# Sliding-window attention by whole chunks in single PSUM banks, in a one-layer encoder step on one core

## The chip, the cores and the metric

The kernel runs on one core of one Trainium2 chip. A core has TensorE (PE in the profile, with its weight loads as PEld), VectorE (DVE), ScalarE (ACT), GpSimd (POOL) and SyncE (SP), on-chip memory for operands, and PSUM, the memory that TensorE writes, which this kernel divides into eight banks of 512 float32 values for each of 128 partitions. Each engine works through its own queue in order; DMA transfers are issued from such queues and run beside them. The metric is the device time of one execution, in microseconds (us).

## The reference

One layer of a hybrid encoder, in float32, over 1088 tokens: 1024 of a prompt and 64 new ones (the "sample"), width 1024. Two branches read one projection: retention (4 heads of 256) and sliding-window attention (SWA). Their gated sum is projected and added; then come cross-attention to 256 memory tokens and a SwiGLU network of width 2816. The part that matters here is the SWA of the mixer:

```python
def swa_attend(q, k, v, bias, sinks, valid):   # chunks of 64 queries; 16 heads in 2 groups; head width 64
    s = einsum('bnqhgd,bnkhd->bnhgqk', q, k) * (SWA_HD ** -0.5)
    s = s + bias                                # own chunk and the two before it: 192 keys
    if valid is not None:
        s = where(valid, s, NEG_INF)
    sink = sinks[:, :, None, None]
    m = maximum(max(s, axis=-1, keepdims=True), sink)
    e = exp(s - m)
    p = e / (sum(e, axis=-1, keepdims=True) + exp(sink - m))
    return einsum('bnhgqk,bnkhd->bnqhgd', p, v)

def merge_branches(ret_o, ret_g, swa_o, gate_a, gate_b, w_ret_out, w_swa_out, w_mix_out):
    a = (rms_norm(ret_o).reshape(B, S, -1) * silu(ret_g)) @ w_ret_out
    b = swa_o.reshape(B, S, -1) @ w_swa_out
    return (sigmoid(gate_a) * a + sigmoid(gate_b) * b) @ w_mix_out
```

There are 17 chunks of 64 queries, 16 of the prompt and one of the sample, whose keys come from a cache. The first two chunks have 64 and 128 keys, all others 192. `mem_kv` also makes the memory's values (`mv`), which are an output.

## The kernel before

`Kernel.run` goes through phases: the projection (with retention and the memory's keys and values beside it), `swa_phase`, `merge_swa`, cross-attention and the SwiGLU network. Large products are made in three fp32r matmuls: an operand is cut by `split` (L122) into a high part, cast by ScalarE (L123), and a low part, subtracted by VectorE (L124), and `mm3` (L153) multiplies high by high, high by low and low by high. In the profile these are the lines L156, L157 and L158. Matmuls of the attention are plain fp32 ones.

**The SWA stage**, `swa` (L927), runs from about 808 to 1000 us. A chunk's 16 heads go in two halves `hf`; in each half there are four tiles, `units`, `(v, i)`: v is the group of keys (two sets of 64 partitions), i the pair of heads. The stage has three steps:

- `scores(c, hf)` (L964): four fp32 products (L972; eight records, since the profile counts two for an fp32 matmul) into `pss`, a tile of two banks with one bank for each v; four VectorE reductions (L982) that add bias and find the row's extreme (`nm`); the sink's term `es` (L986); four ScalarE exponentials with row sums (L988) and one of the sink (L990); then VectorE adds (L991) and inverts (L992) the sums `den`, and GpSimd multiplies the probabilities by them: `t` (L994) for the first 128 keys, `e` (L999, two instructions) for the last 64.
- `turn(c, hf)` (L1003): values are transposed (L949, once per block of keys) into a `pd` bank and copied by ScalarE (L951); four transposes of `t` (L1011) into a bank `pt0`, copied out by ScalarE (L1015, `pT`); two transposes of `e` (L1022) into a bank `pt1`, copied out by VectorE (L1024).
- `weigh(c)` (L1028): eight fp32 products (L1035) of probabilities and values into `pout`, which VectorE copies to `osb` (L1039). Every second chunk is stored to `d_swa`.

PSUM's eight banks are used so: two for `pd` (one-bank tiles of the filler and the value transposes), two for `pss`, one `pt0`, one `pt1`, two `pout`.

**The filler.** Softmax work of VectorE, ScalarE and GpSimd takes longer than the products of a half, so TensorE is given other work between the steps: `filler` (L1151) makes pieces of 12 fp32r matmuls. The first four pieces finish the last head of the memory's values (`wq` by `ms`, 256 columns, scaled by ScalarE at L1167 and stored from GpSimd's queue at L1168 and L1169). All others are halves of a product of retention's output with `w_ret_out` (`ret` by `wq`; 384 columns for the first two blocks of tokens, 320 for the last), multiplied by a gate on VectorE (L1196). The `ret` operands come in three blocks of columns: block 0 was loaded and cast ahead, with its low parts made by `first_low` (L1116, L1120); blocks 1 and 2 are loaded, cast and subtracted by `later_operands` (L1122) in halves of four, when the filler reaches the steps in `extra`.

**What sets the order.** `in_order` (L911) fixes TensorE's order to that of the calls. The loop over half chunks i calls `weigh` of the chunk that ended with half i−1, `scores` of half i+2, `turn` of half i, and then one filler piece (at a few steps two). The other engines' queues are filled by a scheduler that simulates the program's times; `issue_after` and `high_priority` push single instructions. `marks` keeps, for each half, the instructions behind which `first_low` and `later_operands` are to stand.

Of the kernel before, what the change touches and what calls it, by code (L numbers as in the profile page):

```python
# [11 lines left out]
F32 = mybir.dt.float32  # L12
# [97 lines left out]
class Kernel:  # L110
# [781 lines left out]
    def swa_phase(self):  # L892
        with ExitStack() as ctx:
            filler = []

            def fill():


                pieces = self.filler()
                yield []  # L900
# [26 lines left out]
    def swa(self, ctx, fill):  # L927
        nc, tc, io = self.nc, self.tc, self.io
        if True:
# [15 lines left out]
            def values(lo):  # L945
                if lo not in vtok:
                    n = min(P, KC - lo)
                    pt = self.dense_psum()
                    self.last_mm = nc.tensor.transpose(pt[:n, :P], vT[:, lo:lo + n], self.ident).ins  # L949
# [6 lines left out]
            halves = [(c, hf) for c in range(17) for hf in range(2)]  # L956
# [7 lines left out]
            def scores(c, hf):  # L964
                ks, j0, nk = keys(c)
                if hf == 0 and c % 4 == 0 and 0 < c < 13:
                    self.load_queries(qTs, c + 4)
                qT = qTs[c // 4 % 2]
                pss = pw.tile([P, 2, 512], F32, tag="s", name="pss")
                for i in range(2):  # L970
                    for v in range(2):
                        self.last_mm = mm(pss[:, v, i * NKEY:i * NKEY + nk], qT[rows[v], 2 * hf + i, c % 4, :],  # L972
# [4 lines left out]
                ps = pss[:, :, :2 * NKEY].rearrange("p v (i n) -> p v i n", n=NKEY)  # L977
                bs = bias.rearrange("p (v h i) n -> p v h i n", v=2, h=2)
                nm = sw.tile([P, 2, 2], F32, tag="nm", name="nm")
                for v, i in units:  # L980
                    u = quad(self.minus)[:, v, i:i + 1]
                    nc.vector.tensor_tensor_reduce(t[:, v, i, :nk], ps[:, v, i, :nk], bs[:, v, hf, i, j0:], -0.125, u,  # L982
# [20 lines left out]
            def turn(c, hf):  # L1003
                ks, j0, nk = keys(c)
                if hf == 0:
                    live[c] = [values(ks + k0) for k0 in ((0, 64, P) if nk == NKEY else (0,))]
                (t, e), vt = live.pop((c, hf)), live[c]
                n = min(P, nk)
                pp = pw.tile([P, 512], F32, tag="pt0", name="pp")
                for j, (v, i) in enumerate(units):  # L1010
                    self.last_mm = nc.tensor.transpose(pp[:n, j * P:(j + 1) * P], t[:, v, i, :n], self.ident).ins  # L1011
                if hf == 0:
                    live[c, "T"] = [self.pw2.tile([P, 2, 512], F32, tag="pT0", name="pT"), self.pw2.tile([P, 512], F32, tag="pT1", name="pT")]
                pT = live[c, "T"][0][:n]
                nc.scalar.copy(pT[:, :, hf * 256:(hf + 1) * 256], pp[:n, :].rearrange("p (v i) -> p v i", v=2))  # L1015
                cs = [slice(h * 256, (h + 1) * 256) for h in range(2)]
                parts = [[(h, v, vt[0][:n], pT[:, v, cs[h]]) for h in range(2) for v in range(2)]]
                if nk == NKEY:
                    pp = pw.tile([P, 512], F32, tag="pt1", name="pp")
                    for i in range(2):  # L1020
                        x = e[:, i].rearrange("p r k -> p (r k)")
                        self.last_mm = nc.tensor.transpose(pp[:, i * P:(i + 1) * P], x, self.ident).ins  # L1022
                    pT = live[c, "T"][1]
                    nc.vector.tensor_copy(pT[:, hf * 256:(hf + 1) * 256], pp[:, :256])  # L1024
                    parts.append([(h, r ^ h, vt[2 - r][rows[r]], pT[rows[r], cs[h]]) for h in range(2) for r in (h, 1 - h)])
                live[c, "parts"] = parts

            def weigh(c, hf):  # L1028
                if hf == 0:
                    return  # L1030
                parts = live.pop((c, "parts"))
                po = pw.tile([P, 2, 512], F32, tag="out", name="pout")
# [14 lines left out]
            n = len(halves)  # L1047
            for i in range(-2, n):
                if i > 0:
                    self.in_order(lambda: weigh(*halves[i - 1]))  # L1050
                if i + 2 < n:
                    self.in_order(lambda: scores(*halves[i + 2]))
                if i >= 0:
                    self.in_order(lambda: turn(*halves[i]))
                for pieces in next(fill):
                    self.in_order(lambda: next(pieces, None))
                if i == -2:
                    with tc.high_priority(), tc.issue_after(self.last_operand):
                        self.tokens(vT, 1, "cvT")
                if i == 2:  # L1060
                    with tc.issue_after(self.last_operand):
                        self.load_queries(qTs, 4)
                if i == 8:
                    with tc.issue_after(self.last_operand):
                        keep()
            self.in_order(lambda: weigh(*halves[n - 1]))
            for pieces in next(fill):
                self.in_order(lambda: next(pieces, None))
# [82 lines left out]
    def filler(self):  # L1151

        nc, tc, io = self.nc, self.tc, self.io
        if True:
# [3 lines left out]
            for t in range(2):  # L1158
# [7 lines left out]
                with tc.high_priority():  # L1166
                    self.values_out = nc.scalar.mul(o, ps[:, :256], self.mtok[:, t:t + 1]).ins  # L1167
# [9 lines left out]
            extra = {2: (1, 0), 3: (1, 1), 5: (2, 0), 7: (2, 1)}  # L1177
            step = 0
            for m, c in order:
# [9 lines left out]
                for ps in self.pieces(u, rets, c0, n):  # L1189
                    if step in extra:  # L1190
                        i, j = extra.pop(step)
                        self.later_operands(*CH[i], halves[j])
# [641 lines left out]
```

## Time and profile before

| what | value |
|---|---|
| median of 3 runs | 2181.84 us (2179.26 to 2182.01) |
| profiled execution | 2183.19 us |
| its span in the trace | 2181.1 us |
| granted TensorE clock, mean | 0.995 |
| TensorE busy | 2142.3 us, 98% |
| VectorE, ScalarE, GpSimd busy | 1553.4, 876.4, 651.7 us |

A row of the timeline has the start, the duration as recorded, the engine, the line, the operation with its result and operands, the size, how many equal instructions in a row it stands for (x8), and in square brackets the idle time before it and what ended that. Records of one engine overlap a little, since an instruction starts before the one ahead of it has quite ended; the cost of one in a row of many is the distance between starts.

### The profile page before, as it was taken

To read this page: it belongs to the slowest core of one execution; us is meant where nothing else is said; L and a number is where in the kernel's file an instruction comes from. 1 tells how busy PE (TensorE), PEld (TensorE's weight loads), DVE (VectorE), ACT (ScalarE), POOL (GpSimd) and SP (SyncE) were. 2 spreads that over 40 slices of the span, in tenths; PEclk is the share of its full clock that TensorE was granted. 3 is DMA by queue.
4 is the path that set the end of the run, shared out by engine and by line. 5 is a ranking of instruction groups with operands and counts; after the bars stand their busy time and mean duration, and the time that the engine had idled before them with its cause. 6 is when DMAs were issued, how large, how long until landed. Compare 5 with 4: busy or idle time off the path is not lost. (4 is left out here: it accounts for less than half of the span.)

```text
span 2181.1 us, 41848 instructions
## 1 busy us (share of the span) xinstructions
PE 2142.3 (98%) x16389; PEld 2089.0 (96%) x16389; DVE 1553.4 (71%) x2824; ACT 876.4 (40%) x1898; POOL 651.7 (30%) x498
## 2 busy tenths in 40 slices
PE   8999999999999999999999999999999999999997
PEld 8999999999999997889999999999999999999997
DVE  8996868776687658665455555768777777787688
ACT  7344424344344447553233333333322322344343
POOL 1223233342344214430000000014565555514531
PEclk9999999999999999999999999999999999999999
DMA  6434354435344467326443111422333323294433
GB/s 208 154 131 114 114 152 125 137 111 159 103 160 164 166 206 246 118 80 219 124 155 120 40 49 59 146 87 91 121 124 116 105 96 120 94 331 128 135 107 119
DMA packets 181446, 290.84 MB, mean 133 GB/s; under 512 B 40290, under 2 KB 109314, under 8 KB 181250
## 3 DMA queue, kind: packets, MB, share of 16 engines
q1 hardware_dynamic: 176130, 278.18, 40.1%
q10 hardware_dynamic: 4608, 8.36, 1.0%
q8 instruction: 129, 2.11, 0.4%
q0 software_dynamic: 512, 1.64, 0.2%
q14 instruction: 67, 0.55, 0.1%
HBM read 196.95 MB, written 91.16 MB: 132 GB/s over the span
## 5 line engine op out<-in xcount | busy, mean ns | idle before, releaser
L124 DVE TENSOR_TENSOR wq<-raw,wq 128x512 fp32r<-128x512 f32 (+1 forms) x499 | 443.9, 893 | 134.8 <-ACT wq L123 131.4
L123 ACT CAST wq<-raw 128x512 fp32r<-128x512 f32 (+1 forms) x499 | 303.1, 614 | 567.1 <-PE pq L215 223.3
L212 PE MATMUL pq<-T,wq 128*128 128x272 f32 x1832 | 492.0, 288 | 4.9 <-ACT wq L123 3.3
L213 PE MATMUL pq<-T,wq 128*128 128x272 f32 x1832 | 492.9, 289 | 0.0
L213 PE MATMUL pq<-B,wq 128*128 128x272 f32 x1592 | 428.2, 289 | 2.9 <-DVE B L124 2.6
L212 PE MATMUL pq<-B,wq 128*128 128x272 f32 x1592 | 426.6, 288 | 0.5 <-ACT B L123 0.5
L190 POOL TENSOR_TENSOR raw<-raw 128x512 f32<-128x512 f32 (+1 forms) x59 | 86.0, 1458 | 1036.5 <-DVE rs_r L301 483.0
L215 PE MATMUL pq<-T,wq 128*128 128x272 f32 x1832 | 382.8, 289 | 1.5 <-DVE wq L124 1.5
L212 PEld LDWEIGHTS pq<-T,wq 128*128 128x128 f32 x1832 | 345.0, 188 | 6.7 <-ACT wq L123 3.1
L213 PEld LDWEIGHTS pq<-T,wq 128*128 128x128 f32 x1832 | 344.9, 188 | 1.2 <-issue 1.1
L215 PE MATMUL pq<-B,wq 128*128 128x272 f32 x1592 | 332.2, 289 | 0.0
L213 PEld LDWEIGHTS pq<-B,wq 128*128 128x128 f32 x1592 | 299.5, 188 | 4.3 <-DVE B L124 4.2
L212 PEld LDWEIGHTS pq<-B,wq 128*128 128x128 f32 x1592 | 299.4, 188 | 1.4 <-ACT B L123 0.9
L215 PEld LDWEIGHTS pq<-T,wq 128*128 128x128 f32 x1832 | 290.2, 190 | 2.6 <-DVE wq L124 1.8
L215 PEld LDWEIGHTS pq<-B,wq 128*128 128x128 f32 x1592 | 252.2, 190 | 0.5 <-issue 0.4
L259 DVE TENSOR_TENSOR u<-pq,u 128x544 f32<-128x544 f32 x177 | 127.2, 719 | 95.5 <-PE pq L215 95.4
L193 POOL TENSOR_TENSOR raw<-raw 128x512 f32<-128x512 f32 (+1 forms) x59 | 80.8, 1370 | 91.4 <-DVE wq L124 81.5
L598 DVE TENSOR_TENSOR stage<-pq,u 128x544 f32<-128x544 f32 x112 | 80.3, 717 | 36.9 <-PE pq L215 32.4
L191 POOL TENSOR_TENSOR raw<-raw 128x512 f32<-128x512 f32 (+1 forms) x59 | 88.8, 1505 | 3.6
L196 POOL TENSOR_TENSOR raw<-raw 128x512 f32<-128x512 f32 (+1 forms) x59 | 84.0, 1423 | 4.4
L1483 POOL TENSOR_TENSOR stage<-stage,rstd_f 128x544 f32<-128x544 f32 x40 | 63.9, 1607 | 39.1 <-ACT stage L1482 39.1
L156 PE MATMUL pd<-xc,wq 128*128 128x256 f32 (+1 forms) x256 | 74.5, 291 | 0.0
(383 smaller groups left out, 4548.4 us busy)
## 6 DMA issues: line engine op xcount, KB each, us to landing
hl<-d_op SPq DMA_DIRECT2D x85, 272.0 KB, 5.3
d_qkv<-stage SPq DMA_DIRECT2D x44, 272.0 KB, 2.7
d_op<-stage SPq DMA_DIRECT2D x44, 272.0 KB, 2.1
d_op<-ht SPq DMA_DIRECT2D x44, 272.0 KB, 3.3
raw<-w_gate SPq DMA_DIRECT2D x22, 512.0 KB, 3.6
raw<-w_up SPq DMA_DIRECT2D x22, 512.0 KB, 4.0
raw<-w_down SPq DMA_DIRECT2D x16, 512.0 KB, 4.8
d_gate<-stage ACTq DMA_DIRECT2D x28, 272.0 KB, 3.0
```

The costliest lines, as they stand in the source:

```text
L123: self.last_cast = self.nc.scalar.copy(hi, src).ins
L124: return self.nc.vector.tensor_tensor(out=lo, in0=src, in1=hi.bitcast(F32), op=ALU.subtract).ins
L156: mm(ps, wh, xh, start=start, stop=False)
L190: tt(out=a11, in0=a11, in1=a21, op=sub)
L191: tt(out=a21, in0=a21, in1=a22, op=add)
L193: tt(out=a11, in0=a22, in1=a11, op=sub)
L196: tt(out=a12, in0=a12, in1=a11, op=sub)
L212: mm(ps[:, c, :HC], w[:, 0, ks], x[:, 0, cs], start=start, stop=False)
L213: mm(ps[:, c, :HC], w[:, 0, ks], x[:, 1, cs], start=False, stop=False)
L215: self.last_mm = mm(ps[:, c, :HC], w[:, 1, ks], x[:, 0, c * HC:(c + 1) * HC], start=False, stop=stop).ins
L259: add = lambda out, a, b: nc.vector.tensor_tensor(out=out, in0=a, in1=b, op=ALU.add)
L598: nc.vector.tensor_tensor(out=o, in0=ps, in1=sb, op=ALU.add)
```

## The change

The stage goes by whole chunks instead of half chunks.

- *Scores in single banks.* `pss` becomes one tile of one bank for each v, from a ring of four "s" banks. A chunk's two halves take four tiles.
- *Turning.* The transposes of `t` take two more tiles of the same ring, one for each half; those of `e` go into the upper halves of the two banks of the chunk's `pout` tile, whose lower halves `weigh` writes. So `pt0` and `pt1` are gone, and `pout` is taken by `turn`. `e` is copied out once for a chunk instead of once for each half.
- *Values.* All new blocks of a chunk are transposed into one `pd` bank and then copied.
- *Order.* Scores(0), six pieces; then for each chunk c weigh(c−1), scores(c+1), the filler's pieces, turn(c), the filler's pieces. Before, a piece followed each half.
- *Copies first.* The copies by ScalarE out of the banks get high priority, and `marks` takes turn's copies, so that casts for the next columns stand behind them.
- *Filler.* The scaling of the memory's values goes from ScalarE to VectorE. Both halves of column block 1 are requested at step 3 instead of one each at steps 2 and 3.
- The loads of queries for chunks 4 to 7 and the storing of keys and values (`keep`) are called behind chunks 1 and 4.

In the changed program's queues, as built, TensorE has the same instructions. Four gate loads stand ahead of a query load on SyncE's queue. On GpSimd's the issues of the memory values' four stores stand ahead of the first chunk's normalising. On VectorE's the two scalings stand ahead of chunk 0's reciprocals, and the reciprocals of chunk 2 stand behind the reductions of chunk 3.

```diff
-            def values(lo):
-                if lo not in vtok:
-                    n = min(P, KC - lo)
+            def values(los):
+                new = [lo for lo in los if lo not in vtok]
+                if new:
                     pt = self.dense_psum()
-                    self.last_mm = nc.tensor.transpose(pt[:n, :P], vT[:, lo:lo + n], self.ident).ins
-                    vt = vtok[lo] = vts.pop(0)
-                    nc.scalar.copy(vt[:n, :], pt[:n, :P])
-                return vtok[lo]
+                    for j, lo in enumerate(new):
+                        n = min(P, KC - lo)
+                        self.last_mm = nc.tensor.transpose(pt[:n, j * P:(j + 1) * P], vT[:, lo:lo + n], self.ident).ins
+                    for j, lo in enumerate(new):
+                        n = min(P, KC - lo)
+                        vt = vtok[lo] = vts.pop(0)
+                        with tc.high_priority():
+                            nc.scalar.copy(vt[:n, :], pt[:n, j * P:(j + 1) * P])
+                return [vtok[lo] for lo in los]
...
-                pss = pw.tile([P, 2, 512], F32, tag="s", name="pss")
+                pss = [pw.tile([P, 512], F32, tag="s", bufs=4, name="pss") for v in range(2)]
...
+            def turn(c):
...
+                def most(hf):
+                    pp = pw.tile([P, 512], F32, tag="s", bufs=4, name="pp")
+                    t = live[c, hf][0]
+                    for j, (v, i) in enumerate(units):
+                        self.last_mm = nc.tensor.transpose(pp[:n, j * P:(j + 1) * P], t[:, v, i, :n], self.ident).ins
+                    with tc.high_priority():
+                        copied = nc.scalar.copy(first[:, :, cs[hf]], pp[:n, :].rearrange("p (v i) -> p v i", v=2)).ins
+                    self.marks.append((self.marks[-1][0], copied))
+                for hf in range(2):
+                    self.in_order(lambda: most(hf))
+                po = pw.tile([P, 2, 512], F32, tag="out", name="pout")
+                for hf, i in units if nk == NKEY else ():
+                    x = live[c, hf][1][:, i].rearrange("p r k -> p (r k)")
+                    self.last_mm = self.in_order(lambda: nc.tensor.transpose(po[:, hf, (2 + i) * P:(3 + i) * P], x, self.ident)).ins
...
+                    nc.vector.tensor_copy(rest.rearrange("p (h i) -> p h i", h=2), po[:, :, 256:])
...
-            n = len(halves)
-            for i in range(-2, n):
-                if i > 0:
-                    self.in_order(lambda: weigh(*halves[i - 1]))
-                if i + 2 < n:
-                    self.in_order(lambda: scores(*halves[i + 2]))
-                if i >= 0:
-                    self.in_order(lambda: turn(*halves[i]))
-                for pieces in next(fill):
-                    self.in_order(lambda: next(pieces, None))
...
+            self.in_order(lambda: scores(0))
...
+            filled()
+            for c in range(17):
+                if c:
+                    self.in_order(lambda: weigh(c - 1))
+                if c < 16:
+                    self.in_order(lambda: scores(c + 1))
+                filled()
+                self.in_order(lambda: turn(c))
+                filled()
...
-                    self.values_out = nc.scalar.mul(o, ps[:, :256], self.mtok[:, t:t + 1]).ins
+                    self.values_out = nc.vector.tensor_scalar(o, ps[:, :256], self.mtok[:, t:t + 1], None, ALU.mult).ins
...
-            extra = {2: (1, 0), 3: (1, 1), 5: (2, 0), 7: (2, 1)}
+            extra = {3: ((1, 0), (1, 1)), 5: ((2, 0),), 7: ((2, 1),)}
```

More of the change, by code (lines that the diff above doesn't have):

```diff
@@ new lines, in turn, with weigh @@
+                parts = [[(h, v, vt[0][:n], first[:, v, cs[h]]) for h in range(2) for v in range(2)]]
+                if nk == NKEY:
+                    rest = self.pw2.tile([P, 512], F32, tag="pT1", name="pT")
+                    nc.vector.tensor_copy(rest.rearrange("p (h i) -> p h i", h=2), po[:, :, 256:])
+                    parts.append([(h, r ^ h, vt[2 - r][rows[r]], rest[rows[r], cs[h]]) for h in range(2) for r in (h, 1 - h)])
+                live[c] = parts, po
+            def weigh(c):
+                parts, po = live.pop(c)
@@ L1190, in filler @@
                     if step in extra:
[L1191 to L1192 removed]
+                        for i, j in extra.pop(step):
+                            self.later_operands(*CH[i], halves[j])
                     step += 1
```

58 lines of the change are left out of this document (19 added, 39 removed).

## The prediction

> **What bounds the kernel now.** I read the page's busy times first, then the two windows tables over the stage that the change touches, then the timelines of TensorE and of the engines that feed it.
>
> ```profile
> PE 2142.3 (98%) x16389; PEld 2089.0 (96%) x16389; DVE 1553.4 (71%) x2824; ACT 876.4 (40%) x1898; POOL 651.7 (30%) x498
> 800.00:820.00 20.00, 18.17 (x131) 17.70 (x130) 9.57 (x31) 11.83 (x35) 2.23 (x4) 0.83 0.77 199
> 820.00:840.00 20.00, 18.13 (x122) 14.97 (x121) 17.75 (x59) 12.35 (x43) 5.78 (x8) 1.00 0.79 276
> 840.00:860.00 20.00, 19.33 (x142) 15.61 (x142) 17.28 (x65) 15.41 (x55) 8.96 (x13) 1.00 0.87 271
> 900.00:920.00 20.00, 20.00 (x156) 16.39 (x155) 12.86 (x56) 11.40 (x44) 7.41 (x13) 1.00 0.24 75
> ```
>
> A window's columns are its length, the busy us of TensorE, its weight loads, VectorE, ScalarE and GpSimd, the granted clock, the DMA share and GB/s. TensorE bounds the kernel. Within the sliding-window stage (808 to 1000 us) it loses time only in the first 52 us; from 860 on it is full. In 820 to 860 VectorE is busy 35.03 of 40 us, so there VectorE's queue decides what TensorE can have. The first chunks and the full ones are therefore two sums.
>
> **The change, the first chunks.** I follow the start of weigh(c), the products of chunk c with its values. Before:
>
> ```profile
> 809.31 0.66 PE L972 MATMUL pss<-swin,swin 64*128 64x64 f32 x8 [0.82 <-DVE stage L598]
> 810.99 1.12 PE L972 MATMUL pss<-swin,swin 64*128 64x64 f32 x8 [1.01 <-DVE nm L982]
> 812.03 0.58 PE L156 MATMUL pd<-wq,ms 128*128 128x256 f32 x1
> 817.88 0.28 PE L157 MATMUL pd<-wq,ms 128*128 128x256 f32 x1
> 820.27 0.44 PE L156 MATMUL pd<-ret,wq 128*128 128x384 f32 x1
> 825.28 0.71 PE L972 MATMUL pss<-swin,swin 64*128 64x128 f32 x8
> 832.58 1.08 PE L1035 MATMUL pout<-pT,swin 64*64 64x256 f32 x8
> 838.59 0.92 PE L972 MATMUL pss<-swin,swin 64*128 64x192 f32 x8 [1.40 <-DVE nm L982]
> 851.38 1.68 PE L1035 MATMUL pout<-pT,swin 128*64 128x256 f32 x16
> 860.50 1.68 PE L1035 MATMUL pout<-pT,swin 128*64 128x256 f32 x16
> 819.76 0.46 ACT L1167 ACTIVATE swin<-pd,mtok 128x256 f32<-128x256 f32 x1
> 820.51 0.58 POOL L1168 DMA_DIRECT2D d_mv<-swin  x1 [0.97 <-ACT swin L1167]
> ```
>
> Removed at the start: with four single banks the second half's scores no longer wait for the first half's reductions (1.01), nor, later, for 838.59's 1.40. The 48 products of the last value matrix take 8.24 us (812.03 to 820.27), most of them at a step of 0.21, a dip of the clock (0.83 on average in 800 to 820) that follows idle 0.82 and 1.01; at the step after it (20 from 817.88 to 820.27, 0.12 each) they are 5.6. Without the second wait I let the dip not come: −2.6. Scores 809.3 to 810.7, products from 810.9, the first ret piece at 816.5 instead of 820.27. The two pieces there took 5.0 (820.27 to 825.28); 24 products of 384 columns at 0.12 × 1.5 and a change to scores of 0.27 (below) are 4.5, so their fp32r low parts (VectorE L1120) were some 0.5 late; they now come directly behind both halves' reductions, and that goes: −0.5. Then scores(1) at 820.7 for 1.3, one piece of 2.2, turn(0) at 824.2 with its transposes, one piece, weigh(0) at 827.5: 5.1 ahead of 832.58.
>
> Two ScalarE scalings (L1167, 0.46) become VectorE instructions of about 0.4 (nearest: VectorE's copy of 128x256 further below, 0.42; between 0.2 and 0.8). They stand in VectorE's queue before both chunk-0 reciprocals, on the path to turn(0): 0.8 between the end of the exponentials, 819.2, and the reciprocals, 821.75 (with two weight splits of 0.6 each). The issues of the four mv stores (0.58 each, 2.3) now stand in GpSimd's queue ahead of chunk 0's normalising; it starts at about 822.5 and turn(0) is at 824.2: covered, and without cover the 2.3 would lie before turn(0) once. On SP's queue four gate loads pass a query load wanted at chunk 4's scores: nothing, and without that cover something like the longest wait above, 1.40.
>
> What is late next is VectorE. Its rows:
>
> ```profile
> 828.06 0.40 ACT L988 ACTIVATE t<-t,nm 128x128 f32<-128x128 f32 x1
> 833.15 1.74 ACT L123 CAST ret<-swin 128x384 fp32r<-128x384 f32 x4
> 834.40 2.31 DVE L124 TENSOR_TENSOR ret<-swin,ret 128x384 fp32r<-128x384 f32 x3
> 831.92 1.01 DVE L124 TENSOR_TENSOR ret<-swin,ret 128x384 fp32r<-128x384 f32 x2
> 836.63 0.41 DVE L982 CUSTOM_DVE_ANT_0 t<-pss,swin,minus 128x192 f32<-128x192 f32 x1
> 836.97 0.08 DVE L982 DVE_READ_ACCUMULATOR2_ANT nm<- 128x1 f32 x1
> 843.37 0.68 DVE L1039 COPY osb<-pout 128x512 f32<-128x512 f32 x1
> 842.22 0.56 DVE L1196 TENSOR_TENSOR swin<-pd,swin 128x384 f32<-128x384 f32 x1 [0.92 <-PE pd L158]
> 919.13 0.69 DVE L124 TENSOR_TENSOR wq<-raw,wq 128x512 fp32r<-128x512 f32 x1
> 839.86 1.04 POOL L994 TENSOR_TENSOR t<-t,den 128x512 f32<-128x512 f32 x1 [4.03 <-DVE den L992]
> 840.86 0.76 POOL L999 TENSOR_TENSOR e<-t,den 128x128 f32<-128x128 f32 x2
> ```
>
> A low part costs 0.5 alone and 0.77 when GpSimd runs beside it, a reduction of 192 columns 0.34 (836.63 to 836.97). All eight low parts of the second column block now come at one step, behind ScalarE's casts (0.44 each), and those, by the new marks, behind chunk 0's copies out of the banks.
>
> *Stall A, turn(1).* The transposes take "s" banks that scores(2) must have left. TensorE is there at 828.5 (after weigh(0)) + 1.6 scores + 2.2 piece = 832.3. The banks come free thus: reciprocals of chunk 0 821.75, a gate product 0.5, eight reductions(1) of 0.27 to 824.4, the exponentials behind them (0.40 recorded) to 826.05, three copies to 827.1, the first cast 827.5. From there VectorE's queue (the changed program's order) has seven lows at 0.57 (between 0.5 and 0.77), a gate product 0.5 and weigh(0)'s copy-out 0.6: 832.6, then two reductions, 833.3 (first bank), an eighth low and two more, 834.5 (second). Stall 1.0 + 0.9 = 1.9. Weigh(1) at 837.3.
>
> *Stall B, turn(2).* TensorE is there at 842.5. But turn(2) needs chunk 2's reciprocals, and in VectorE's new queue these stand behind the gate product that ends with the piece at 837.5, four lows of 320 columns (320/384 of 0.57), weigh(1)'s copy-out, two weight splits and the reductions of chunk 3: 0.48 + 4 × 0.5 + 0.6 + 2 × 0.7 + 8 × 0.34 + small ones 0.3 = 7.4, to 844.9. GpSimd then takes 1.04 + 0.76 for the first half and as much for the second, to 848.5. Stall 3.5 + 1.3 = 4.8; with every low at 0.77 and GpSimd at the 1.04 alone, between 3 and 6.5. Turn(2) ends at 848.7, weigh(2) starts at 850.95 against 851.38, weigh(3) at 859.5 against 860.50 (which had lost 0.49). The first chunks give −1.0 without the clock; nearly all of the 5.1 goes back to VectorE.
>
> *The clock.* What idling does here:
>
> ```profile
> 46.00:48.00 2.00, 0.00 (x0) 0.00 (x0) 2.00 (x3) 0.55 (x3) 1.92 (x2) 1.00 1.04 385
> 48.00:50.00 2.00, 1.86 (x13) 1.86 (x14) 2.00 (x4) 1.41 (x4) 1.17 (x1) 0.88 1.02 383
> 50.00:52.00 2.00, 2.00 (x10) 2.00 (x10) 2.00 (x4) 2.00 (x5) 0.00 (x0) 0.50 0.16 45
> 52.00:54.00 2.00, 2.00 (x14) 2.00 (x14) 1.90 (x4) 0.78 (x2) 0.00 (x0) 0.77 0.86 304
> ```
>
> Some 2 us without work (46 to 48) are followed by about 3.4 us at half clock (0.12, 0.50 and 0.23 of 2 us lost), worth 1.7; the pair 0.82 + 1.01 by the longer dip worth 2.6; the single 1.40 ahead of 838.59 by none (820 to 860 has 1.00). Stall B is longer than all of these: a dip, +1.7. Stall A, 1.9, is like both the 2 us and the pair, but in two parts with work between: half of 1.8, +0.9. Together +2.6.
>
> The Trainium skill, page "TensorE: Matmul & The Clock Gate", section "Part 1: The HAM clock gate", has the array fall to half clock after at least one idle window of about 3.4 us, and rise after as long a busy one. The dip of 3.4 us agrees with the second half of that; the dip after about 2 us idle does not agree with the first, and the trace decides. By that rule stall A would not dip and stall B would.
>
> **The change, the full chunks.** Per chunk the products, transposes and two pieces are the same; only their order changes.
>
> ```profile
> 973.69 0.34 PE L158 MATMUL pd<-ret,wq 128*128 128x384 f32 x1
> 973.96 0.87 PE L1035 MATMUL pout<-pT,swin 128*64 128x256 f32 x6
> 978.30 0.34 PE L158 MATMUL pd<-ret,wq 128*128 128x384 f32 x1
> 978.47 0.27 PE L949 MATMUL pd<-ident,swin 128*128 128x128 f32 x1
> 917.94 1.68 PE L1035 MATMUL pout<-pT,swin 128*64 128x256 f32 x16
> 927.13 1.68 PE L1035 MATMUL pout<-pT,swin 128*64 128x256 f32 x16
> 917.53 0.42 DVE L1024 COPY pT<-pp 128x256 f32<-128x256 f32 x1
> 921.60 0.57 ACT L1015 COPY pT<-pp 128x512 f32<-128x512 f32 x1
> ```
>
> A chunk takes 9.19 (917.94 to 927.13, with pieces of 384). A piece followed by fp32 products costs 0.27, one followed by a transpose 0.17: a chunk used to leave its two pieces into fp32 products both times, now once into products and once into transposes: −0.10, and one change fewer between transposes and scores about −0.07. Over 13 full chunks −2.2 (bounds: −1.2 if scores to piece costs more than now, −2.6 if each change saves 0.2). The merged copies of the e transposes (two of 0.42 to one of 512 columns, 0.69 at most) relieve VectorE by 0.15; VectorE is not the bound there, nothing.
>
> The cover: the pT copies (2 × 0.48) and the rest copy now all lie behind turn(c) with one piece, 2.25 or 1.94, before weigh(c) uses them. From the scores' start: reductions begin at 0.9, the eight exponentials take ScalarE to 5.2 (0.45 each, 3.6, begun behind the first reduction and held up once by VectorE), turn's transposes end at 4.9, the two pT copies at 6.5, and weigh is due at 6.95 (1.7 + 1.94 + 1.4 + 1.94): slack 0.45. Casts stand behind the copies in ScalarE's queue. If the slack is used up, TensorE waits by what is missing, in each chunk.
>
> Sum: −1.0 + 2.6 − 2.2 = −0.6. The profiled execution (2183.19, span 2181.1) would become 2182.6; it is 1.35 above the median of 2181.84, which becomes 2181.2.
>
> **Rivals.**
> *Stall B does not arise*, because VectorE runs ahead of my sum by what TensorE gained at the start (its low parts at 0.5, not 0.77). Then −5.1 + 1.9 for A − 2.2 = −5.4: 2176.4. For it: twelve lows at 0.2 less each are 2.4; against: the reciprocals of chunk 2 stand behind chunk 3's reductions whatever the durations.
> *The copies are late in each full chunk* (the other side). Place: weigh waits for the second pT copy. It decides from 0.45 of delay; VectorE's and ScalarE's queues vary by a split of 0.69 and a cast of 0.57. At 0.5 a chunk × 13 = +6.5, with the sum 2187.7. Against: VectorE is busy 12.86 of 20 there, ScalarE 11.40.
> *Longer dips*: both stalls dip as at 811 (2.6 each) and last 2.5 longer together: −1.0 + 5.2 + 2.5 − 2.2 = +4.5: 2186.3.
> *Only stall B dips*: −1.0 + 1.7 − 2.2 = −1.5: 2180.3. For it, the 1.40 that did not dip; against, the pair 0.82 + 1.01. This is the case that the Trainium skill's clock-gate rule gives.
> *The change does nothing*: scores to turn costs come back elsewhere and the lead of 5 us dies in VectorE's queue wholly: 2181.8.
>
> **How the numbers follow.** Less than 0.2% (4.4 us) a measurement of this kernel can hardly tell from no change. My sum 0.37, only B 0.14, nothing 0.05: within 0.2%, 0.56. No stall B 0.20: faster. Late copies 0.18 and longer dips 0.06: slower, 0.24. The range takes in the no-stall case, 2176.4, and the late copies, 2187.7; the likeliest case's own is 2178 to 2184.5.
>
> **What would show it.** Right: second scores half without a wait at 810; clock 1.00 in 812 to 818; weigh(0) near 827.5; TensorE waiting at turn(1) for reductions and at turn(2), 842 to 848, for GpSimd; clock 0.5 behind that; weigh(3) 859.5 plus the dips; 9.0 a full chunk. Wrong: a wait of weigh for ScalarE in every chunk, or full TensorE from 840 on.

## The result, and the profile after

The changed kernel takes 2185.54 us (median of 20 runs, 2179.12 to 2188.42) against 2180.96 (20 runs, 2178.06 to 2186.32): a ratio of 1.0017, 95% interval 1.0010 to 1.0024. It is slower by about 3.7 us, less than 0.2%, where 0.03% faster was forecast. Single executions of either kernel differ by several us, which matters for what follows: the first trace of the changed kernel is of its fastest execution (2179.12), and the one trace of the kernel before on which the prediction rests is of an execution 2.2 above the median of 20 (2183.19).

The page's line of busy times, after:

```profile
PE 2135.6 (98%) x16389; PEld 2088.9 (96%) x16389; DVE 1558.7 (72%) x2811; ACT 871.3 (40%) x1896; POOL 646.3 (30%) x498
```

TensorE's share is the same 98%; where it is idle shows in the windows of the attention stage (columns as before: length, TensorE, weight loads, VectorE, ScalarE, GpSimd, clock, DMA share, GB/s):

```profile
800.00:820.00 20.00, 17.63 (x147) 16.80 (x145) 14.97 (x47) 11.86 (x34) 4.96 (x9) 1.00 0.92 296
820.00:840.00 20.00, 18.59 (x129) 15.77 (x127) 16.24 (x64) 16.80 (x62) 2.04 (x2) 1.00 0.64 207
840.00:860.00 20.00, 15.60 (x113) 12.88 (x115) 14.05 (x52) 11.25 (x43) 11.28 (x18) 0.91 0.69 219
```

The clock no longer falls in the first window; the idle time has moved to 840 to 860, and the clock falls there. TensorE's timeline, the rows that answer to those of before (L979 is L972 before, L1020 is L1011, L1044 is L1035, L1178 is L1167):

```profile
806.01 1.11 PE L979 MATMUL pss<-swin,swin 64*128 64x64 f32 x16 [0.82 <-DVE stage L598]
814.54 0.41 PE L156 MATMUL pd<-ret,wq 128*128 128x384 f32 x1 [1.55 <-DVE swin L1178]
825.33 1.08 PE L1044 MATMUL pout<-pT,swin 64*64 64x256 f32 x8
831.00 0.63 PE L1020 MATMUL pp<-ident,t 128*128 128x128 f32 x4 [0.81 <-DVE nm L988]
832.15 0.63 PE L1020 MATMUL pp<-ident,t 128*128 128x128 f32 x4 [0.52 <-DVE nm L988]
834.80 1.08 PE L1044 MATMUL pout<-pT,swin 128*64 128x256 f32 x8
843.12 0.66 PE L1020 MATMUL pp<-ident,t 128*128 128x128 f32 x4 [3.20 <-POOL t L1000]
844.84 1.03 PE L1020 MATMUL pp<-ident,t 128*128 128x128 f32 x4 [1.06 <-POOL t L1000]
849.57 1.68 PE L1044 MATMUL pout<-pT,swin 128*64 128x256 f32 x16
858.11 1.68 PE L1044 MATMUL pout<-pT,swin 128*64 128x256 f32 x16 [0.22 <-DVE pT L1036]
```

This trace starts its stage 3.3 us earlier than that of before (806.01 against 809.31). Nothing here ties that to the change, so from here on times count from the first scores. Weigh(0) comes at 19.3 instead of 23.3, weigh(1) at 28.8 instead of 32.8, weigh(2) at 43.6 instead of 42.1: the lead of 4 us is gone within one chunk, at turn(2), where TensorE waits 3.20 and 1.06 for GpSimd. GpSimd itself waits for chunk 2's reciprocals (L998), which VectorE comes to directly behind the last reduction of chunk 3 (L988; the timelines of VectorE and GpSimd; as what ended GpSimd's idle time the profile names L992, a small VectorE instruction right behind them):

```profile
841.30 0.42 DVE L988 CUSTOM_DVE_ANT_0 t<-pss,swin,minus 128x192 f32<-128x192 f32 x1
841.71 0.24 DVE L998 RECIPROCAL den<-den 128x4 f32<-128x4 f32 x2
842.03 1.04 POOL L1000 TENSOR_TENSOR t<-t,den 128x512 f32<-128x512 f32 x1 [16.14 <-DVE es L992]
```

Behind the wait the clock goes, as windows of 2 us show:

```profile
844.00:846.00 2.00, 1.16 (x6) 1.17 (x7) 0.00 (x0) 0.56 (x2) 2.00 (x4) 0.75 1.06 285
846.00:848.00 2.00, 2.00 (x9) 2.00 (x8) 1.25 (x2) 1.92 (x5) 2.00 (x4) 0.50 1.00 350
848.00:850.00 2.00, 2.00 (x12) 1.65 (x13) 2.00 (x4) 0.00 (x0) 1.42 (x3) 0.90 1.06 392
```

0.25, 0.50 and 0.10 of 2 us each are 1.7 us lost. The measure of the stage used below is the time from the first scores to the first product of the next phase: 191.57 in the trace of before, 190.93 here. By these two traces the change gains 0.64 us, which is nearly the sum that was forecast; by the runs it loses 3.7. The experiments had first to find out which of the two is the rule.

### The profile page after: what moved, and what is told of

It is laid out like the page before. It is cut to its first block, busy times and chain, and to the rows that moved or that the text cites. A ratio compares the mean times of both kernels' runs of the same rounds, so it can differ in the third digit from the quotient of the medians.

```text
span 2177.1 us, 41827 instructions
## 1 busy us (share of the span) xinstructions
PE 2135.6 (98%) x16389; PEld 2088.9 (96%) x16389; DVE 1558.7 (72%) x2811; ACT 871.3 (40%) x1896; POOL 646.3 (30%) x498
## 3 DMA queue, kind: packets, MB, share of 16 engines
q0 software_dynamic: 512, 1.64, 0.2%
## 4 chain that ended last, share of the span: by engine, by line
PE 83%; DVE 8%; DMA 3%; ACT 3%; issue 2%; POOL 1%; SPq 0%; POOLq 0%; DVEq 0%; ACTq 0%
PE pq L215 17%; PE pq L212 17%; PE pq L213 17%; PE pd L156 8%; PE pd L158 7%; PE pd L157 7%; DVE wq L124 2%; PE pout L1044 1%; PE pss L979 1%; ACT t L994 1%; DMA raw<-w_down 1%; DMA d_qkv<-stage 1%; DVE t L988 1%; PE pk L736 1%; DMA raw<-w_k 1%
## 5 line engine op out<-in xcount | busy, mean ns | idle before, releaser
L994 ACT ACTIVATE t<-t,nm 128x192 f32<-128x192 f32 (+2 forms) x136 | 58.9, 434 | 57.9 <-DVE nm L988 57.9
```

## Experiments

Two theories stood against each other. Q: the loss lies in the attention stage, in waits that VectorE's queue makes in the first chunks and in clock dips behind them, whose length differs from execution to execution. E: the stage is as the first trace has it, and the loss lies outside.

**More traces of both kernels.** The kernel before, three times more, and the changed kernel, three times more; no edit.

> The kernel before, once more, for a second trace of it. Theory Q (the loss lies in the attention stage, in the waits of the first chunks and the clock dips behind them): weigh(16) starts 174.3 us after the first scores, within 1 us, as in the first trace; the dip behind the first two waits may be of another length, by up to 2 us. Theory E (the loss lies elsewhere, in executions that differ outside the stage): the stage repeats, and the time outside it differs by several us between the two traces.

> The changed kernel as it is, for a second trace and a time beside the others. Its first trace (2179.12) is of an execution 6 us faster than the median of 2185.54. Both theories: ratio 1.001 to 1.0025. Theory Q: a trace of an execution near the median shows the same waits at the same places, but a clock below 1.00 behind more of them, or longer, so that weigh(16) comes 3 to 6 us later after the first scores than the 173.9 of the first trace. Theory E: weigh(16) at 173.9 within 1 us, and the 3 to 6 us lie before or behind the stage.

> The kernel before, for a third trace: how long is the clock dip behind the first two waits as a rule? In the two traces so far TensorE ran at half clock for 6.4 and for 3.4 us there (3.0 and 1.7 us lost), and chunk 0's values products started 23.3 and 21.2 us after the first scores. Theory Q (the dips come in lengths of about 3.4 us or twice that, once per stall or pair of stalls): 1.7 or 3.0 lost again, weigh(0) at 21.2 or 23.3, weigh(4) at 59.8 or 61.8. Theory E (the time of the changed kernel is lost outside the stage): the dip is there as well, and the time from the stage's end to the last instruction is under 1181.

> The kernel before, a fourth trace, for the same question: weigh(0) at 21.2 or 23.3 after the first scores if a dip of one of the two lengths comes each time; about 19.5 if it is sometimes absent, in which case the kernel before is faster as a rule than its first trace says.

> The changed kernel, a third trace: the dip behind turn(2) was 3.4 us in the first (1.7 lost) and 6.8 in the second (3.4 lost). Theory Q: one of the two again, weigh(16) at 173.9 or at 174.6 to 175.6 after the first scores, and no other dip in the stage. Theory E: the stage's end at 191 to 191.7 as before, and over 1182 from there to the last instruction.

> The changed kernel, a fourth trace, and a time beside the other runs. Theory Q: weigh(16) at 173.9 to 175.6 after the first scores, a dip of 1.7 or 3.4 us behind turn(2) and none elsewhere in the stage; ratio 1.0005 to 1.0025.

The repeats of the changed kernel had ratios of 1.0008 (0.9999 to 1.0018) and 1.0016 (1.0006 to 1.0026); the other was a single execution. Lost clock is the sum over 2 us windows of what the granted clock lacks to 1.00. It is not the same as lost time: in the third trace of after the clock is at 0.50 in a window that begins 0.6 us before the wait at turn(2) ends, and half clock costs nothing while TensorE waits. From the first scores:

| trace | weigh(0) | weigh(4) | weigh(16) | stage end | clock lost, and where |
|---|---|---|---|---|---|
| before, first | 23.27 | 61.82 | 174.33 | 191.57 | 3.4, first scores |
| before, second | 21.19 | 59.78 | 172.30 | 189.38 | 1.7, first scores |
| before, third | 21.07 | 59.62 | 172.14 | 189.21 | none |
| before, fourth | 22.05 | 60.62 | 173.14 | 190.22 | 3.4, first scores |
| after, first | 19.32 | 63.50 | 173.86 | 190.93 | 1.7, turn(2) |
| after, second | 19.13 | 64.10 | 174.62 | 191.69 | 3.4, turn(2) |
| after, third | 19.19 | 63.77 | 174.18 | 191.25 | 3.4, turn(2) |
| after, fourth | 21.55 | 66.84 | 177.23 | 194.46 | 1.7, first ret piece; 3.4, turn(2) |

The stage ends at 190.1 on average before and 192.1 after: +2.0. So the stage holds 2.0 us of loss, as Q has it. The first trace of before had the longest stage of its four, the first trace of after the shortest. Outside the stage the traces scatter by 2 to 5 us: from the stage's end to the last instruction 1180.2 to 1184.7 before and 1180.2 to 1185.1 after, both ends alike. Ahead of the stage, the first scores come at 808.75 on average before and 806.58 after, so that the whole spans of the eight traces average 2181.85 and 2181.95: as wholes they do not show the loss of the runs. All four traced executions of before lie above its medians (2182.89 to 2186.16 against 2180.96 to 2181.91), and no trace ties the 2.2 us ahead of the stage to the change. These traces alone therefore don't exclude E; the edits below speak for Q, since they change the stage and the time follows.

The third trace of before shows what the dip at its first scores is worth. In it the clock stays up, and TensorE waits for ScalarE instead (TensorE's timeline):

```profile
809.58 0.66 PE L972 MATMUL pss<-swin,swin 64*128 64x64 f32 x8 [1.01 <-DVE nm L982]
816.67 0.44 PE L156 MATMUL pd<-ret,wq 128*128 128x384 f32 x1 [0.56 <-ACT swin L1167]
828.98 1.08 PE L1035 MATMUL pout<-pT,swin 64*64 64x256 f32 x8
```

Weigh(0) is at 21.07 without a dip, 21.19 with 1.7 lost and 22.05 to 23.27 with 3.4 lost. The last of these, on which the prediction rests, is late for another reason, which rows of ScalarE, VectorE and TensorE show, first the first trace and then the third:

```profile
808.54 2.58 ACT L1108 CAST ret<-swin 128x384 fp32r<-128x384 f32 x5 [5.36 <-DMA swin<-d_gate]
817.92 0.16 DVE L991 TENSOR_TENSOR den<-den,es 128x4 f32<-128x4 f32 x1 [6.79 <-ACT es L990]
827.03 0.41 PE L156 MATMUL pd<-ret,wq 128*128 128x384 f32 x1 [0.35 <-DVE swin L1196]
804.59 2.62 ACT L1108 CAST ret<-swin 128x384 fp32r<-128x384 f32 x5 [2.81 <-DMA swin<-d_gate]
814.33 0.16 DVE L991 TENSOR_TENSOR den<-den,es 128x4 f32<-128x4 f32 x1 [4.61 <-ACT es L990]
823.44 0.41 PE L156 MATMUL pd<-ret,wq 128*128 128x384 f32 x1 [0.34 <-DVE swin L1196]
```

The ret product waits for a bank that VectorE's gate product L1196 reads. VectorE comes to that late because it waited for ScalarE's exponentials, and these stand behind casts that began when their DMA had landed: 0.8 us ahead of the first scores in the first trace, 3.3 in the third. In the first three traces weigh(0) comes 5.54 to 5.55 behind this ret product (17.72, 15.64 and 15.53 from the first scores), whatever was lost of the clock. In the fourth there is no such wait, and TensorE's own delay counts: 22.05, 1.0 behind the trace without a dip. So a dip at the start of the kernel before cost between nothing and 1.0 us.

The fourth trace of after shows the other end: a wait of 2.22 for the scaling, and a dip behind it (0.75, 0.50 and 0.90 in the windows of 816 to 822) besides that of turn(2). The timelines of ScalarE, VectorE and TensorE there:

```profile
805.15 2.62 ACT L1119 CAST ret<-swin 128x384 fp32r<-128x384 f32 x5 [3.76 <-DMA swin<-d_gate]
816.01 0.16 DVE L997 TENSOR_TENSOR den<-den,es 128x4 f32<-128x4 f32 x1 [0.59 <-ACT es L996]
816.09 0.87 DVE L1178 TENSOR_SCALAR swin<-pd,mtok 128x256 f32<-128x256 f32 x2
816.72 0.41 PE L156 MATMUL pd<-ret,wq 128*128 128x384 f32 x1 [2.22 <-DVE swin L1178]
```

Read upwards: the ret product waits for a pd bank that the scaling L1178 has yet to read; the scaling stands on VectorE behind the sums L997 of chunk 0, those wait for ScalarE's exponentials, and these stand behind casts that began 2.4 us ahead of the first scores (805.15 against 807.52) because their DMA landed then. In the first trace of after the same casts (ScalarE's timeline) began 3.6 ahead of the scores, and the wait was 1.55:

```profile
802.42 2.62 ACT L1119 CAST ret<-swin 128x384 fp32r<-128x384 f32 x5 [2.55 <-DMA swin<-d_gate]
```

In the seven traces in which VectorE scales behind chunk 0's sums (those of the changed kernel and three of the edits below), the wait grows with the start of the last of the eight casts: 1.36 where that is 0.94 or 1.07 behind the first scores, 1.55 at 1.38, 1.80 to 1.91 at 1.64 to 1.72, 2.22 at 2.05.

**Chunk 2's reciprocals first.** One order added: on VectorE chunk 3's reductions stand behind chunk 2's reciprocals.

```diff
-                    nc.vector.tensor_tensor_reduce(t[:, v, i, :nk], ...
+                    with tc.issue_after(live["recip"]) if c == 3 else ExitStack(): nc.vector.tensor_tensor_reduce(t[:, v, i, :nk], ...
...
-                nc.vector.reciprocal(den, den)
+                live["recip"] = nc.vector.reciprocal(den, den).ins
```

> The changed kernel with one order more: chunk 3's reductions on VectorE stand behind chunk 2's reciprocals. Theory Q: the waits of turn(2) for GpSimd (3.20 and 1.06 in the trace of the changed kernel) shrink to under 1.5 in all, the half clock behind them goes, weigh(2) comes 4 to 6 us earlier after the first scores than 43.6, and the time falls by 4 to 6 us against the changed kernel: ratio to the kernel before 0.998 to 0.9997. Theory E: the wait goes, but the ratio stays at 1.0005 or above.

Measured 2180.46, ratio 0.9995 (0.9985 to 1.0005), 3.25 under the changed kernel on the same chip (2183.71). TensorE's timeline at turn(2):

```profile
842.82 0.66 PE L1020 MATMUL pp<-ident,t 128*128 128x128 f32 x4 [0.48 <-POOL t L1000]
844.55 0.66 PE L1020 MATMUL pp<-ident,t 128*128 128x128 f32 x4 [1.08 <-POOL t L1000]
847.73 1.68 PE L1044 MATMUL pout<-pT,swin 128*64 128x256 f32 x16
```

The first wait shrinks from 3.2 to 0.48, the granted clock is 1.00 in every window of the stage, weigh(2) is at 39.56 instead of 43.6 to 46.8, the stage ends at 187.48. Without stall B and its dip the stage is thus 2.6 shorter than the mean of before instead of 2.0 longer; the ratio's interval still takes in 1. The waits left are 1.56 in all, where Q had under 1.5, and the time fell by 3.25, where Q had 4 to 6.

**And the scaling ahead of chunk 0's sums.** The same, and the first scaling goes ahead of the last five low parts; the sums, reciprocals and normalising of chunk 0, kept in `waiting` until then, go behind it.

```diff
-    def first_low(self):
+    def first_low(self, part, after):
-        with self.tc.issue_after(self.marks[-1][0]):
-            for a, hi, lo in self.first:
+        with self.tc.issue_after(after):
+            for a, hi, lo in self.first[part]:
...
-            self.first_low()
+            self.first_low(slice(0, 5), self.marks[-1][0])
...
                     self.values_out = nc.vector.tensor_scalar(o, ps[:, :256], self.mtok[:, t:t + 1], None, ALU.mult).ins
+                if t == 0: self.first_low(slice(5, 10), self.values_out)
+                with tc.issue_after(self.values_out):
+                    while self.waiting: self.waiting.pop(0)()
```

> As the run before it, and the scaling of the first half of the memory's values goes ahead of the last five low parts and of chunk 0's sums on VectorE, so that TensorE finds its pd bank free for the first ret piece (1.55 us of waiting in the changed kernel's trace). Theory Q: that wait goes or falls under 0.5, weigh(0) comes 1.0 to 1.6 earlier, and the time is up to 1.6 below that of the run with the reciprocals alone; if the low parts then are late for the first ret products, the gain shrinks to 0.5. Theory E: no difference between the two runs that can be told.

Measured 2176.84, ratio 0.9980 (0.9969 to 0.9991), 6.9 under the changed kernel beside it: faster than both kernels. In the timelines of VectorE and TensorE the first scaling comes at 812.54, the ret products follow without a wait, and of the larger waits only those of turn(1) and turn(2) are left:

```profile
812.54 0.48 DVE L1180 TENSOR_SCALAR swin<-pd,mtok 128x256 f32<-128x256 f32 x1
814.15 0.28 PE L158 MATMUL pd<-wq,ms 128*128 128x256 f32 x1
814.27 0.34 PE L156 MATMUL pd<-ret,wq 128*128 128x384 f32 x1
830.66 0.63 PE L1022 MATMUL pp<-ident,t 128*128 128x128 f32 x4 [0.81 <-DVE nm L988]
```

Weigh(0) is at 17.53, the stage ends at 185.07, 7.0 under the changed kernel's mean of 192.1, which is the 6.9 of the times. Against the run before it the time falls by 3.6, more than the 1.6 expected; the traces differ by 2.4, of which 2.0 lie ahead of weigh(0), where a wait of 1.80 went, and 0.35 between weigh(4) and weigh(16).

**Column block 1 in two steps.** The same, with the first four operands of block 1 requested two steps earlier.

```diff
-            extra = {3: ((1, 0), (1, 1)), 5: ((2, 0),), 7: ((2, 1),)}
+            extra = {1: ((1, 0),), 3: ((1, 1),), 5: ((2, 0),), 7: ((2, 1),)}
```

> As the run with both edits, and the first four operands of column block 1 are requested at step 1 of the filler instead of all eight at step 3, so that their casts and low parts fall in the stretch in which VectorE stood idle (2.84 us ahead of the first gate product). Theory Q (stall A is the eight low parts at one step): the waits of turn(1) for the reductions, 0.81 and 0.52, go, and as the later steps move up, weigh(4) comes at 55.5 to 56.5 instead of 57.45, with 0.998 falling to 0.9975. Rival (the loads are not there so early, or the casts now delay the second scaling): TensorE waits 1 to 2 us at the second or third ret piece, and nothing is gained.

Measured 2177.28, ratio 0.9976 (0.9963 to 0.9988), on another chip than the run with both edits alone; the stage ends at 185.11, as without the edit. From the list of what TensorE waited for in the stage:

```profile
PE pout L1046 <- DVE pT L1038: 1.3, 3, 0.6
PE pout L1046 <- ACT pT L1024: 0.9, 2, 0.5
PE pp L1022 <- DVE nm L988: 0.5, 2, 0.3
```

Turn(1)'s waits for the reductions, 1.33 in all, are gone; the two left in the list are of turn(0) (0.30) and turn(2) (0.24). So the eight low parts at one step did cause stall A. But weigh(0) comes 1.2 later (18.77) and weigh waits for ScalarE's copies; weigh(4) is at 57.43 against 57.45. Neither Q's gain nor the rival's wait at the ret pieces came: the stall is only exchanged for others.

**Useless work in the place of stall B.** The changed kernel with products that nobody reads while it waits at turn(2).

```diff
+                po = pw.tile([P, 2, 512], F32, tag="out", name="pout")
+                for i in range(24 if c == 2 else 0):
+                    x = self.rets[0][:, 0, :256]
+                    self.last_mm = self.in_order(lambda: mm(po[:, 0, 256:], x[:, :P], x, start=True, stop=True)).ins
...
                 def most(hf):
...
-                po = pw.tile([P, 2, 512], F32, tag="out", name="pout")
                 for hf, i in units if nk == NKEY else ():
```

> The changed kernel with 24 products of no use (128x128 by 128x256, into the part of the pout banks that the e transposes overwrite) ahead of turn(2)'s transposes of t, in the time in which TensorE waits for GpSimd there. The queues of the other engines are unchanged, so the stall stays, filled with work; only the clock can answer. Theory Q (idle time at turn(2) starts the dip): no granted clock below 1.00 behind turn(2), the idle time before t's first transposes falls from 3.2 to 0 to 0.4, weigh(2) at 41.7 to 42.3 instead of 43.6 to 44.2, weigh(16) 1.7 to 3.4 earlier, ratio 0.999 to 1.0008. Rival (the dip has another cause, or the products come too late and push turn(2) back): the dip stays, or weigh(2) is no earlier than 43.5.

TensorE's timeline at turn(2):

```profile
842.77 2.32 PE L1019 MATMUL pout<-ret 128*128 128x256 f32 x18
845.42 0.66 PE L1025 MATMUL pp<-ident,t 128*128 128x128 f32 x4 [0.34 <-POOL t L1000]
847.13 0.66 PE L1025 MATMUL pp<-ident,t 128*128 128x128 f32 x4 [1.05 <-POOL t L1000]
850.31 1.68 PE L1048 MATMUL pout<-pT,swin 128*64 128x256 f32 x16
```

And the windows behind it:

```profile
846.00:848.00 2.00, 0.94 (x8) 0.79 (x8) 0.00 (x0) 0.76 (x2) 2.00 (x5) 1.00 0.98 258
848.00:850.00 2.00, 2.00 (x14) 2.00 (x13) 1.68 (x3) 1.85 (x5) 2.00 (x4) 1.00 1.02 302
```

t's transposes come no earlier, GpSimd being what they wait for, but the clock stays at 1.00: weigh(2) at 42.43 although weigh(0) was late (19.77) in this trace, stage end 190.01. From weigh(1) to weigh(2) it takes 13.2 against 14.8 to 15.8 in the four traces of the changed kernel. Measured 2182.15, ratio 1.0004 (0.9995 to 1.0013), 3.6 under the changed kernel beside it (2185.71); the intervals of the two ratios still overlap. Nothing was edited but this idle time, and the dip is gone. So idle time of TensorE starts the dip, and the dip alone is worth 1.6 to 2.6 us by the traces, 2.1 on average.

**Without the copies' priority.** The changed kernel without the two priorities and the mark.

```diff
-                        with tc.high_priority():
+                        with ExitStack():
...
-                    with tc.high_priority():
+                    with ExitStack():
...
-                    self.marks.append((self.marks[-1][0], copied))
```

> The changed kernel without its priority for ScalarE's copies and without the marks, so that in the first chunks the casts of the next columns stand ahead of the copies out of the banks. Theory Q (ScalarE's order decides nothing in the full chunks but does in the first): weigh(0) 3 to 4 us later than 19.2, since eight casts of 0.44 stand ahead of its pT copies; the reductions then come earlier by as much or not at all, stalls A and B grow or move, stage end 1 to 4 us later than 191.3; the full chunks from weigh(4) to weigh(16) within 0.4 of 110.4. Rival (VectorE alone binds the first chunks): weigh(0) is late, weigh(2) is not, stage end within 0.5.

Measured 2184.47, ratio 1.0010 (1.0001 to 1.0019). Neither theory's forecast held: weigh(0) is 2.4 to 2.6 late against three of the four traces (21.72), weigh(1) at 32.91, but weigh(2) is earlier (42.48), and TensorE never waits for GpSimd; the stage ends at 189.92. That the casts in front let VectorE run ahead is the likely reason, which no run here shows by itself. From the list of what TensorE waited for in the stage:

```profile
PE pout L1043 <- ACT pT L1022: 4.7, 3, 2.0
PE pd L156 <- DVE swin L1177: 1.8, 1, 1.8
PE pout L1043 <- DVE pT L1035: 1.0, 4, 0.5
```

Stalls A and B (5.6 in all) are exchanged for waits of weigh for ScalarE (4.7 in three pieces, the first of 1.96 followed by a dip of 1.7). The full chunks are the same: weigh(4) to weigh(16) 110.33. So putting copies first is worth nothing in the full chunks and moves the loss in the first ones.

**The scaling back on ScalarE.** The changed kernel with this part undone.

```diff
-                    self.values_out = nc.vector.tensor_scalar(o, ps[:, :256], self.mtok[:, t:t + 1], None, ALU.mult).ins
+                    self.values_out = nc.scalar.mul(o, ps[:, :256], self.mtok[:, t:t + 1]).ins
```

> The changed kernel with the scaling of the memory's values back on ScalarE, the one part undone. The wait of TensorE for the scaling (1.36 to 1.55 with VectorE) has two possible causes. Rival (VectorE was the wrong engine): the wait falls under 0.3 and weigh(0) comes 1.3 earlier. Theory Q (either engine reaches the scaling only behind chunk 0's exponentials, which end at 7.7 after the first scores): a wait of 1.0 to 1.5 remains, weigh(0) within 0.4 of 19.2, stage end within 0.5 for equal dips.

TensorE's timeline at the first ret piece:

```profile
817.69 0.44 PE L156 MATMUL pd<-ret,wq 128*128 128x384 f32 x1 [2.68 <-ACT swin L1178]
```

The wait did not go; it was 2.68 here, longer than Q's 1.0 to 1.5, in an execution whose casts began only 2.2 ahead of the first scores. One execution doesn't say that ScalarE is worse; it says that the engine was not the cause. The place in the queue was, behind chunk 0's exponentials or their sums: with VectorE's scaling moved ahead of them, above, no wait was left.

## Why the prediction was wrong, and where it was right

*The start.* "Without the second wait I let the dip not come: −2.6" and "weigh(0) at 827.5: 5.1 ahead of 832.58" failed twice. The dip did not come, but it was not what held weigh(0) in the trace that was read: there VectorE was late, behind casts whose DMA landed late, and in the kernel before a dip cost between nothing and 1.0. The other three traces of before have weigh(0) at 21.07 to 22.05. Against the mean of before, 21.9, the changed kernel's 19.1 to 21.6 (mean 19.8) is ahead by 2.1, not 5.1.

*The scaling.* "They stand in VectorE's queue before both chunk-0 reciprocals, on the path to turn(0): 0.8" followed the scaling's result and not its operand. The bank that it reads is wanted by the first ret piece, and TensorE waited 1.36 to 2.22 for it in the changed kernel, in the longest case with a dip of 1.7. From that piece on TensorE reaches weigh(0) without a further wait, 10.8 us later (12.4 with the dip), so the wait counts in full, and with it the DMA that feeds ScalarE's casts.

*Stall A*: 0.81 + 0.52 (0.72 to 0.81, and 0.52, in all four) where 1.9 was forecast, with the cause that was given. No trace has a dip behind it, so nothing came of the +0.9 for half a dip.

*Stall B*: 3.2 and 0.6 to 1.06, where 3.5 and 1.3 were forecast, at the place and for the reason given; the reciprocal behind the reductions proved it when it was moved. Its dip was counted at 1.7. The clock lost there was 1.7 in one trace of four and 3.4 in three, and in time it cost 2.1 on average, so that shorter waits and a longer dip about cancelled.

*The clock.* The Trainium skill's page "TensorE: Matmul & The Clock Gate", section "Part 1: The HAM clock gate", gives a free-running window of about 3.4 us, and half clock after at least one such window without work. The runs agree in the length: what was lost in the stage was 1.7 or 3.4 us and nothing between, half clock for 3.4 us or twice that. They don't agree that 3.4 us without work is needed: waits of 1.96, 2.22 and 2.68 were followed by a dip too, and no single wait of stall B was longer than 3.25. That stall B dipped and stall A did not is what the prediction drew from that rule.

*The full chunks*: −2.2 was forecast over 13 chunks, which are those from weigh(3) to weigh(16). These took 123.1 to 123.2 before and 121.8 to 121.9 after: −1.3. From weigh(4) on the forecast held (112.5 before in all four traces, 110.4 to 110.5 after: −2.1). But weigh(3) to weigh(4) took 11.40 in all four traces of after against 10.63 before, with two waits of TensorE that were counted as nothing: 0.25 for ScalarE's copy of the values, and one for VectorE's merged copy of e (TensorE's timeline of the first trace):

```profile
869.51 1.68 PE L1044 MATMUL pout<-pT,swin 128*64 128x256 f32 x16 [0.50 <-DVE pT L1036]
```

Weigh waits for that copy at chunks 3 and 11 too (0.22 and 0.20). The slack of ScalarE's pT copies held, none of weigh's waits there is for ScalarE.

*The sum.* −0.6 agrees with the first two traces (−0.64) only because errors cancelled and because both traces are from the edges of their kernels: luck. By the means of four traces the stage moved by +2.0, 2.6 more than forecast, in three parts. Weigh(3) of the kernel before is at 49.8 where 51.2 was taken: 1.4. The changed kernel's weigh(3) is at 53.15 where 52.8 was forecast: 0.35, made of 1.6 for weigh(0), ahead of which the wait for the scaling lies, −0.3 between weigh(0) and weigh(1), and −0.9 between weigh(1) and weigh(2), since stall A had no dip. The full chunks lack 0.9. So the failing steps are the price of the dip at the start (2.6 taken, nothing to 1.0 shown, in a kernel before that is as a rule 1.4 ahead of its first trace), the wait for the scaling (1.36 to 2.22, not in the sum), and the waits between weigh(3) and weigh(4), taken for nothing (0.75). The runs moved by 3.7 (1.0010 to 1.0024 of 2181, so 2.2 to 5.2), and in the repeats by ratios of 1.0008 and 1.0016, which are 1.7 and 3.5; what lies between 2.0 and those is not placed by these traces.

*The rivals.* Late copies in each chunk did not come, nor did stall B stay away. "Only stall B dips" is what came, held at 0.14; its 2180.3 still missed, because it took the same gain at the start. The longer dip came behind stall B alone, with the stalls no longer than forecast.

## What to carry to other kernels

A trace is one execution: where a term of the sum is a clock dip or a wait for a DMA, look at several executions of the kernel before, or price it as a chance. Look also at which engine the next step really waits for, since a loss that another engine's chain covers is not to be won. When the order of work changes, follow for each moved instruction both what waits for its result and what waits for the bank it reads. In this stage every single wait of TensorE of 1.96 us or more was followed by half clock besides. The order of two instructions on VectorE and the place of one scaling took this change from 1.0008 to 0.9980 beside it.

## What the runs showed of the hardware

Within the stage, dips came in two sizes, 1.7 or 3.4 us lost. Single waits of 1.36 to 1.91 led to none in ten traces; waits of 1.96, 2.22, 2.68 and 3.2 led to one each time; the pair of 0.82 and 1.01 led to none, to the short or to the long one, in four executions of the kernel before. Work whose result nobody reads kept the clock up: 24 products in a wait of 3.2 us; from weigh(1) to weigh(2) it then took 13.2 us instead of 14.8 to 15.8.
